# Differential attention: the near keys' bias block becomes the last of equal key blocks, and its maximum is taken negated

## The chip, the cores and the metric

The kernel runs on one core of a Trainium2 chip. The metric is the device time of one execution in microseconds; the time before is the median of three timed runs. A separate execution was taken with the hardware profiler, and all the rows shown come from it.

## What is computed

One inference step of a one-layer streaming encoder: a norm, one input projection, two groups of attention heads side by side, an output projection, an MLP with squared ReLU, a gated embedding and a final norm, for a prompt of 2048 tokens and a sample of 32 tokens with 128 cached keys. The change touches group A, the differential attention: 4 heads, each with two maps of 64 dimensions and values of 128.

```python
def diff_core(q, k, v, bias, mask, lam):
    s = jnp.einsum('bqhmd,bkhmd->bhmqk', q, k) * (HEAD_DIM ** -0.5) + bias[:, None]
    s = jnp.where(mask, s, NEG)
    p = jax.nn.softmax(s, axis=-1)
    w = p[:, :, 0] - lam * p[:, :, 1]
    return jnp.einsum('bhqk,bkhe->bqhe', w, v)
```

The mask lets a query see the keys of its own chunk of 64 and of all chunks before. The bias depends on the distance between key and query by buckets (T5), and far enough back all distances share the last bucket, so that there the bias is a constant that drops out of the softmax. The kernel subtracts that constant from the table once; what is left is zero for all keys but the nearest ones.

## The kernel before

**Precision by halves.** Operands are split into a high part and a rest (`hi`, `lo`), each product is three matmuls (`mm3`, L211 to L213), and the rest is computed by GpSimd (POOL, L174 and L184) or VectorE (DVE).

**Tiles.** Queries are taken in 16 tiles of 128 (`t`), two tiles to a pair (`attn_a_pair`). `attn_a` runs over the heads `g`, and for each head loads the bias tile `ba` (`bias_a`: 256 columns, one buffer, the visible corner masked by a POOL memset, L314) and the keys `ka`, then runs over its pairs. It is called four times in the program: twice in a first stretch for tiles 0 to 3 and then tiles 4 to 7 with the sample (`JA0`; `ka` has one buffer there), and twice in a second stretch for tiles 8 to 11 and 12 to 15 (`JA1`).

**Blocks.** The keys that tile `t` sees, 128 (t + 1) of them, are cut into blocks. The last 256 keys (128 for tile 0) are the near block, with the bias; the rest are far blocks of up to 512, as equal as multiples of 128 allow, without bias. For each block and each of the two maps `m`:

- PE computes the scores into one of three PSUM banks `s`, two matmuls, one for each half of q (L594).
- Far block: DVE takes the negated maximum straight from PSUM (L600), ACT the exponential from PSUM with that maximum as its bias, with the sum of the row accumulated in `z` (L608).
- Near block: DVE adds the bias, writes the sum to SBUF and takes the maximum in the same instruction (L603, with a second, short instruction that reads the maximum out), negates the maximum (L606), and ACT takes the exponential from SBUF (L608).

Then the maxima of the blocks are joined, if there is more than one (L613 to L624: a minimum, an exponential on ACT for each map, five short DVE instructions); each block of the second map is scaled by ACT (L630), and added to the first map's scaled block by DVE (L631). PE transposes the result in groups of four 128 x 128 pieces into PSUM (`tpp`, L666), ACT and DVE split it (`pH` L673, `pL` L674), and PE multiplies with the values (`o`, L680 to L682). A norm of the head's output follows (L684 to L694, with `ss` on PE).

**Order.** The instruction order of every engine comes from a scheduler that models the time of each instruction and fills an engine's gaps with later work: in the first stretch with projections (`vps`, `qps`) and the transposes of the prompt (`xp`), in the second with the MLP of the first half of the tokens (`ups`, `dps`; DVE adds `dps` into `h` at L982). The order is fixed in the program, and each engine runs its own in order. All transfers are issued in order from SP's queue (L165).

Of the kernel before, what the change touches and what calls it, by code (L numbers as in the profile page):

```python
# [12 lines left out]
F32 = mybir.dt.float32  # L13
F32R = mybir.dt.float32r
AF = mybir.ActivationFunctionType
ALU = mybir.AluOpType
# [3 lines left out]
P = 128  # L20
D = 1024
SP = 2048
SS = 32
T = SP + SS
PAST = 128
# [4 lines left out]
NEG = -1e30  # L30
# [121 lines left out]
class Kern:  # L152
# [155 lines left out]

    def bias_a(self, pool, h):
        nc = self.nc  # L310
        t = pool.tile([P, 256], F32, tag="ba", bufs=1, name="ba")
        src = self.dba[h, 127 : 127 + P * 383].rearrange("(p c) -> p c", c=383)[:, :256]
        self.dma(t, src)
        nc.gpsimd.memset(t[0:64, 192:256], NEG)  # L314
        return t

    def bias_b(self, pool, h):
# [235 lines left out]
    def attn_a_pair(self, g, j, kt, ba, pool, ps_s, ps_t, ps_o):  # L553
        nc = self.nc
# [9 lines left out]
        for qi, t in enumerate(tiles):  # L564
            if samp:
                nr = SS
                blocks = [(SP, PAST + SS, 0)]
                kb = SP
                nkeys = PAST + SS
            else:  # L570
                nr = P
                kb = 0
                nkeys = P * (t + 1)
                nfar = max(nkeys - 256, 0)
                nb = (nfar + 511) // 512
                blocks = []
                pos = 0
                for i in range(nb):
                    n = P * ((nfar // P - pos // P + nb - i - 1) // (nb - i))
                    blocks.append((pos, n, None))  # L580
                    pos += n
                blocks.append((nfar, nkeys - nfar, 256 - (nkeys - nfar)))
            nb = len(blocks)
            e = [
                pool.tile([P, 2048 if not self.small else 1024], F32, tag=f"e{m}", bufs=2 if m == 0 or self.small else 1, name="e")
                for m in range(2)
            ]
            nm = pool.tile([P, 2, 8], F32, tag="nm", bufs=2, name="nm")
            z = pool.tile([P, 2, 8], F32, tag="z", bufs=2, name="z")
            for bi, (k0, n, near) in enumerate(blocks):  # L590
                for m in range(2):
                    s = ps_s.tile([P, 512], F32, tag="s", name="s")[:nr, :n]
                    for hl in range(2):
                        nc.tensor.matmul(  # L594
                            s, q[:, m, hl, P * qi : P * qi + nr], kt[:, m, k0 - kb : k0 - kb + n], start=hl == 0, stop=hl == 1
                        )
                    dst = e[m][:nr, k0 - kb : k0 - kb + n]
                    nmx = nm[:nr, m, bi : bi + 1]
                    if near is None:
                        nc.vector.tensor_reduce(nmx, s, axis=AX.X, op=ALU.max, negate=True)  # L600
                        src = s
                    else:
                        nc.vector.tensor_tensor_reduce(  # L603
                            dst, s, ba[:nr, near : near + n], 1.0, -3e38, ALU.add, ALU.max, nmx
                        )
                        nc.vector.tensor_scalar(nmx, nmx, -1.0, None, op0=ALU.mult)  # L606
                        src = dst
                    nc.scalar.activation(dst, src, AF.Exp, bias=nmx, accum_out=z[:nr, m, bi : bi + 1])  # L608
            c = pool.tile([P, 2, 8], F32, tag="c", bufs=2, name="c")
            rz = pool.tile([P, 2], F32, tag="rz", bufs=2, name="rz")  # L610
            if nb > 1:
                gm = pool.tile([P, 2], F32, tag="gm", bufs=2, name="gm")
                nc.vector.tensor_reduce(gm[:nr], nm[:nr, :, :nb], axis=AX.X, op=ALU.min)  # L613
                for m in range(2):
                    nc.scalar.activation(
                        c[:nr, m, :nb], nm[:nr, m, :nb], AF.Exp, bias=gm[:nr, m : m + 1], scale=-1.0
                    )
                nc.vector.tensor_tensor(z[:nr, :, :nb], z[:nr, :, :nb], c[:nr, :, :nb], op=ALU.mult)
                nc.vector.tensor_reduce(rz[:nr], z[:nr, :, :nb], axis=AX.X, op=ALU.add)
                nc.vector.reciprocal(rz[:nr], rz[:nr])  # L620
                nc.vector.tensor_scalar(c[:nr, 0, :nb], c[:nr, 0, :nb], rz[:nr, 0:1], None, op0=ALU.mult)
                nc.vector.tensor_scalar(
                    c[:nr, 1, :nb], c[:nr, 1, :nb], rz[:nr, 1:2], self.nlam[:nr], op0=ALU.mult, op1=ALU.mult
                )  # L624
            else:
                nc.vector.reciprocal(c[:nr, :, 0], z[:nr, :, 0])
                nc.vector.tensor_scalar(c[:nr, 1, 0:1], c[:nr, 1, 0:1], self.nlam[:nr], None, op0=ALU.mult)
            for bi, (k0, n, near) in enumerate(blocks):
                sl = slice(k0 - kb, k0 - kb + n)
                nc.scalar.activation(e[1][:nr, sl], e[1][:nr, sl], AF.Copy, scale=c[:nr, 1, bi : bi + 1])  # L630
                nc.vector.scalar_tensor_tensor(  # L631
                    e[0][:nr, sl], e[0][:nr, sl], c[:nr, 0, bi : bi + 1], e[1][:nr, sl], op0=ALU.mult, op1=ALU.add
                )
            ws.append(e[0])
# [7 lines left out]
        for c0 in range(0, len(kts), 4):  # L642
# [16 lines left out]
            for qi, w in enumerate(ws):  # L659
                nr = SS if samp else P  # L660
# [984 lines left out]
```

## Time and profile before

| | |
|---|---|
| median of three timed runs | 3224.73 us (3218.4 to 3230.53) |
| profiled execution | 3224.94 us |
| its span (first to last instruction) | 3223.1 us |
| mean granted PE clock | 0.974 |
| busy: PE, DVE, ACT, POOL | 3019.3, 1813.4, 1791.5, 1768.7 us |
| score matmuls of group A (L594, prompt) | 768 |
| DVE maxima of far blocks (L600) | 256, 147.4 us |
| DVE bias and maximum of near blocks (L603) | 136, 53.7 us |
| negations (L606) | 136 |

A row of the grouped view reads: line, engine, operation, tile written <- tiles read, partitions x elements, count, then busy time in us and the mean in ns of one, then the idle time of the engine right before these instructions and which instruction ended it. A wait row reads: waiting instruction <- what ended the wait, total us, number of times, the longest. Matmuls are pipelined, and the length shown for one includes its way through the array, so what a matmul takes up is read from one start to the next.

### The profile page before, as it was taken

How to read it: one execution, taken by the hardware profiler on the slowest of the kernel's cores; microseconds unless marked ns; L12 is line 12 of the kernel's file. 1: busy time of each engine (PE TensorE's matmuls, PEld its weight loads, DVE VectorE, ACT ScalarE, POOL GpSimd, SP SyncE). 2: the span in 40 equal slices, each digit the busy share in tenths (PEclk: the TensorE clock that was granted, in tenths of full speed). 3: DMA queues.
4: the chain of work that ended last, by engine and by line, in shares of the span. 5: the costliest groups of instructions: out<-in, count | busy, mean ns of one | idle time of the engine just before them, and what ended most of it. 6: DMA issues, size and time to landing. Idle time of an engine off the chain costs nothing.

```text
span 3223.1 us, 51787 instructions
## 1 busy us (share of the span) xinstructions
PE 3019.3 (94%) x17497; PEld 2639.9 (82%) x17497; DVE 1813.4 (56%) x4270; ACT 1791.5 (56%) x3966; POOL 1768.7 (55%) x2451
## 2 busy tenths in 40 slices
PE   7989898999989999999999999998899999999997
PEld 6967788879878888788889999887788887888875
DVE  5126765444455454676675676235466665755845
ACT  4226665666566675676676776334354454444543
POOL 5427657443234544565564445657465567677751
PEclk9989899999999999999999999999999999999998
DMA  7578676987687854654564534456444468675611
GB/s 218 182 198 233 191 210 197 256 235 218 187 243 212 240 146 123 158 174 136 146 190 134 138 110 135 131 163 196 133 153 148 158 242 287 203 253 186 219 58 53
DMA packets 556257, 579.89 MB, mean 180 GB/s; under 512 B 41900, under 2 KB 412912, under 8 KB 555992
## 3 DMA queue, kind: packets, MB, share of 16 engines
q1 hardware_dynamic: 555992, 576.58, 59.7%
q8 instruction: 139, 2.28, 0.3%
q14 instruction: 126, 1.03, 0.1%
HBM read 438.37 MB, written 142.01 MB: 180 GB/s over the span
## 4 chain that ended last, share of the span: by engine, by line
PE 63%; DMA 11%; DVE 9%; ACT 4%; POOL 2%; issue 2%; SPq 1%; DVEq 0%; POOLq 0%; ACTq 0%
PE xps L211 3%; PE xps L212 3%; PE xps L213 3%; PE ups L211 3%; PE ups L212 3%; PE ups L213 3%; PE dps L211 3%; PE s L594 3%; PE dps L212 3%; PE dps L213 3%; PE dp L211 2%; PE dp L213 2%; PE dp L212 2%; PE ob L800 2%; PE gps L213 2%
## 5 line engine op out<-in xcount | busy, mean ns | idle before, releaser
L184 POOL TENSOR_TENSOR wl<-wr,wh 128x256 fp32r<-128x256 f32 x776 | 580.6, 780 | 463.3 <-ACT wh L189 405.4
L189 ACT ACTIVATE wh<-wr 128x1024 fp32r<-128x1024 f32 x258 | 272.6, 1057 | 259.4 <-PE dps L212 40.3
L211 PE MATMUL dps<-uh,wh 128*128 128x272 f32 (+1 forms) x768 | 265.4, 346 | 35.6 <-DVE h L982 27.7
L174 POOL TENSOR_TENSOR wl<-wr,wh 128x256 fp32r<-128x256 f32 x256 | 193.6, 787 | 170.5 <-ACT wh L189 170.3
L211 PE MATMUL ups<-cH,wh 128*128 128x272 f32 (+1 forms) x768 | 250.6, 327 | 2.7 <-ACT sqacc L913 1.5
L213 PE MATMUL dps<-uh,wl 128*128 128x272 f32 (+1 forms) x768 | 252.0, 328 | 0.0
L212 PE MATMUL dps<-ul,wh 128*128 128x272 f32 (+1 forms) x768 | 252.0, 328 | 0.0
L212 PE MATMUL ups<-cL,wh 128*128 128x272 f32 (+1 forms) x768 | 249.8, 325 | 1.2 <-POOL cL L174 1.2
L213 PE MATMUL ups<-cH,wl 128*128 128x272 f32 (+1 forms) x768 | 250.2, 326 | 0.0
L982 DVE TENSOR_TENSOR h<-h,dps 128x272 f32<-128x272 f32 (+1 forms) x384 | 195.9, 514 | 90.9 <-PE dps L213 88.7
L211 PE MATMUL qps<-aH,wh 128*128 128x512 f32 (+1 forms) x640 | 229.3, 358 | 8.8 <-DVE a L368 3.6
L213 PE MATMUL qps<-aH,wl 128*128 128x512 f32 (+1 forms) x640 | 229.0, 358 | 0.0
L212 PE MATMUL qps<-aL,wh 128*128 128x512 f32 (+1 forms) x640 | 228.5, 357 | 0.0
L594 PE MATMUL s<-ka,q 128*128 128x512 f32 (+3 forms) x768 | 188.9, 350 | 37.0 <-ACT e L608 19.3
L211 PEld LDWEIGHTS dps<-uh,wh 128*128 128x128 f32 x768 | 148.5, 193 | 60.6 <-DVE h L982 40.0
L608 ACT ACTIVATE e<-s,nm 128x384 f32<-128x384 f32 (+3 forms) x256 | 154.6, 609 | 64.5 <-DVE nm L600 42.6
L600 DVE TENSOR_REDUCE nm<-s 128x1 f32<-128x512 f32 (+3 forms) x256 | 147.4, 587 | 61.1 <-PE s L594 60.0
L212 PE MATMUL dp<-dx,dw 128*128 128x512 f32 x448 | 177.5, 396 | 0.7 <-DVE dx L195 0.7
L174 POOL TENSOR_TENSOR dw<-dv,dw 128x256 fp32r<-128x256 f32 x160 | 149.2, 961 | 49.1 <-ACT dw L189 39.8
L211 PE MATMUL dp<-dx,dw 128*128 128x512 f32 x448 | 174.7, 396 | 0.0
L594 PEld LDWEIGHTS s<-ka,q 128*128 128x128 f32 x768 | 128.3, 196 | 54.3 <-ACT e L608 24.3
L213 PE MATMUL dp<-dx,dw 128*128 128x512 f32 x448 | 171.5, 396 | 0.0
(273 smaller groups left out, 9593.9 us busy)
## 6 DMA issues: line engine op xcount, KB each, us to landing
wd<-w_down SPq DMA_DIRECT2D x96, 512.0 KB, 5.4
wr<-w_in SPq DMA_DIRECT2D x74, 512.0 KB, 5.5
q<-qS SPq DMA_DIRECT2D x256, 128.0 KB, 4.1
v<-vSa SPq DMA_DIRECT2D x64, 512.0 KB, 4.4
wr<-w_up SPq DMA_DIRECT2D x64, 512.0 KB, 4.3
wr<-w_down SPq DMA_DIRECT2D x64, 512.0 KB, 4.0
ut<-uS SPq DMA_DIRECT2D x56, 512.0 KB, 4.1
ka<-kS SPq DMA_DIRECT2D x32, 512.0 KB, 8.0
```

Of the source, the lines that this page charges most:

```text
L174: nc.gpsimd.tensor_tensor(out[:, sl], a[:, sl], b[:, sl], op=op)
L184: nc.gpsimd.tensor_tensor(out[:, sl], a[:, sl], b[:, sl], op=op)
L189: nc.scalar.activation(hi, raw, AF.Copy)
L211: nc.tensor.matmul(ps, lh, rh, start=start and i == 0, stop=False)
L212: nc.tensor.matmul(ps, lh, rl, start=False, stop=False)
L213: nc.tensor.matmul(ps, ll, rh, start=False, stop=stop and i == n - 1)
L594: nc.tensor.matmul(s, q[:, m, hl, P * qi : P * qi + nr], kt[:, m, k0 - kb : k0 - kb + n], start=hl == 0, stop=hl == 1)
L600: nc.vector.tensor_reduce(nmx, s, axis=AX.X, op=ALU.max, negate=True)
L608: nc.scalar.activation(dst, src, AF.Exp, bias=nmx, accum_out=z[:nr, m, bi : bi + 1])
L800: nc.tensor.matmul(o[:, qa:qb], vt, pt[:kn, i - kfirst, qa:qb], start=x == 0 and y == 0, stop=x == len(order) - 1 and y == 1,)
L982: nc.vector.tensor_tensor(hv, hv, ps, op=ALU.add)
```

## The change

Three edits. The near block is no longer a block of its own of 256 keys: all the keys of a tile are cut into equal blocks of up to 512, and the last of them is the one with the bias. The bias tile grows to 512 columns, its first half zero, set by one more POOL memset; a last block of n keys uses its last n columns. A tile of 512 keys or fewer has one block, and nothing to join.

Per head the blocks of the 16 tiles go from 1, 1, 2, 2, 2, 2, 3, 3, 3, 3, 4, 4, 4, 4, 5, 5 to 1, 1, 1, 1, 2, 2, 2, 2, 3, 3, 3, 3, 4, 4, 4, 4. The near blocks are 128, 256, 384, 512, 256, 384, 384, 512, 384, 384, 384, 512, 384, 384, 384 and 512 wide.

The instruction that adds the bias now also multiplies by -1 and takes the minimum, so that the negated maximum comes out of it, and the separate negation goes. What it writes has its sign turned, which the exponential undoes with a scale of -1.

```diff
     def bias_a(self, pool, h):
-        t = pool.tile([P, 256], F32, tag="ba", bufs=1, name="ba")
+        t = pool.tile([P, 512], F32, tag="ba", bufs=1, name="ba")
         src = self.dba[h, 127 : 127 + P * 383].rearrange("(p c) -> p c", c=383)[:, :256]
-        self.dma(t, src)
-        nc.gpsimd.memset(t[0:64, 192:256], NEG)
+        self.dma(t[:, 256:], src)
+        nc.gpsimd.memset(t[:, :256], 0.0)
+        nc.gpsimd.memset(t[0:64, 448:512], NEG)
         return t
...
-                blocks = [(SP, PAST + SS, 0)]
+                blocks = [(SP, PAST + SS, 256)]
...
-                nfar = max(nkeys - 256, 0)
-                nb = (nfar + 511) // 512
+                nb = (nkeys + 511) // 512
                 blocks = []
                 pos = 0
                 for i in range(nb):
-                    n = P * ((nfar // P - pos // P + nb - i - 1) // (nb - i))
-                    blocks.append((pos, n, None))
+                    n = P * ((nkeys // P - pos // P + nb - i - 1) // (nb - i))
+                    blocks.append((pos, n, None if i < nb - 1 else 512 - n))
                     pos += n
-                blocks.append((nfar, nkeys - nfar, 256 - (nkeys - nfar)))
...
                         nc.vector.tensor_tensor_reduce(
-                            dst, s, ba[:nr, near : near + n], 1.0, -3e38, ALU.add, ALU.max, nmx
+                            dst, s, ba[:nr, near : near + n], -1.0, 3e38, ALU.add, ALU.min, nmx
                         )
-                        nc.vector.tensor_scalar(nmx, nmx, -1.0, None, op0=ALU.mult)
                         src = dst
-                    nc.scalar.activation(dst, src, AF.Exp, bias=nmx, accum_out=z[:nr, m, bi : bi + 1])
+                    nc.scalar.activation(
+                        dst, src, AF.Exp, bias=nmx, scale=1.0 if near is None else -1.0,
+                        accum_out=z[:nr, m, bi : bi + 1],
+                    )
```

Since the scheduler places every instruction anew, the order of all engines moves between the first stretch and the end of the second.

## Prediction

> **What bounds the kernel now.** I read the page first (PE is busy for 94% of the span), then the busy time by stage, then who waited for whom on PE inside the two stages that the change touches. Keys and queries of the differential attention meet in two stretches: heads over tiles 0 to 7 from 222 to 505 us, and over tiles 8 to 15 from 1283 to 1960 us. The busy times of these stages (columns as in the header):
>
> ```profile
> core 0: us, PE busy (x) PEld busy (x) DVE busy (x) ACT busy (x) POOL busy (x), PEclk, DMA share, GB/s
> 222.00:505.00 283.00, 243.82 (x1635) 222.47 (x1636) 199.67 (x680) 192.06 (x593) 168.98 (x258) 0.93 0.76 211
> 1283.00:1960.00 677.00, 644.18 (x3962) 576.90 (x3962) 451.44 (x1047) 461.52 (x1111) 359.85 (x517) 0.98 0.53 147
> ```
>
> PE idles 39 us of 283 in the first and 33 of 677 in the second, while DVE and ACT, the engines that the change relieves, are at two thirds. So the attention is not bound by DVE or ACT: projections and the MLP, scheduled between its steps, keep PE going. What DVE and ACT save reaches the end of the span only through PE's waits. Those of the first stretch, largest first (total us, times, longest):
>
> ```profile
> PE s L594 <- DMA q<-qS: 8.7, 5, 3.6
> PE s L594 <- DMA ka<-kS: 8.4, 2, 4.4
> PE tpp L666 <- DVE e L631: 6.8, 7, 2.2
> PE s L594 <- ACT e L608: 5.2, 8, 1.4
> PE ss L691 <- DVE sh L191: 3.3, 2, 2.0
> PE tpp L666 <- DVE pL L674: 3.2, 2, 2.0
> ```
>
> And of the second:
>
> ```profile
> PE s L594 <- ACT e L608: 14.1, 8, 6.2
> PE dps L211 <- DVE h L982: 9.8, 17, 1.6
> PE o L681 <- DVE pL L674: 3.3, 1, 3.3
> PE dps L211 <- ACT relu L947: 3.1, 3, 2.4
> ```
>
> Two kinds stand there. Loads of q and k: 17.1 us. Waits that end on DVE or ACT: 18.5 us in 19 waits in the first stretch, 30.3 us in 29 in the second, together **48.8 us in 48 waits**. That is all that the change can shorten directly.
>
> **The change part by part.**
>
> *Matmuls.* Per head the 16 tiles have 48 blocks before and 40 after. Times 4 heads, 2 maps and 2 halves that is 128 fewer score matmuls (768 to 640), but the key columns are the same. Does a matmul cost by itself? PE's rows in order of time, from start to next start:
>
> ```profile
> 1940.62 0.40 PE L594 MATMUL s<-ka,q 128*128 128x256 f32 x2
> 1940.85 0.28 PE L680 MATMUL o<-pH,v 128*128 128x256 f32 x1
> ...
> 1941.27 0.27 PE L681 MATMUL o<-pL,v 128*128 128x128 f32 x1
> 1941.38 0.27 PE L682 MATMUL o<-pH,v 128*128 128x128 f32 x1
> ...
> 1946.42 0.63 PE L594 MATMUL s<-ka,q 128*128 128x512 f32 x2
> 1946.89 0.29 PE L211 MATMUL dps<-uh,wh 128*128 128x272 f32 x1
> ```
>
> Two of 256 columns occupy 0.23 us, two of 512 occupy 0.47: 0.45 and 0.46 ns a column, nothing left per matmul. I take 0 for the 128. The bound from the other side is the 128-column row: 0.11 us where its columns are worth 0.06, so 0.05 each, 6.6 us at most; a loss is excluded, as no column is added. The Trainium skill, "TensorE: Matmul & The Clock Gate", section "Back-to-back issue gap", gives a sustained 81 ns at 128 columns and 131 ns at 512, that is some 64 ns that do not depend on width; by it 128 matmuls would be an estimated 8 us. The two pairs above speak against it.
>
> *DVE and ACT.* The durations, by shape (count, then total us and mean ns); L763 is the band attention's instruction of the same kind as L603, and shows widths that L603 does not have yet:
>
> ```profile
> L600 DVE TENSOR_REDUCE nm<-s 128x1 f32<-128x512 f32 x104 | 69.8, 683 | 19.4 <-PE s L594 18.8
> L600 DVE TENSOR_REDUCE nm<-s 128x1 f32<-128x384 f32 x128 | 69.6, 549 | 39.9 <-PE s L594 39.5
> L603 DVE CUSTOM_DVE_ANT_0 e<-s,ba 128x256 f32<-128x256 f32 x120 | 49.0, 418 | 38.4 <-PE s L594 30.2 <-POOL ba L314 4.2 <-issue 2.1
> L606 DVE TENSOR_SCALAR nm<-nm 128x1 f32<-128x1 f32 x128 | 17.9, 147 | 1.0
> L631 DVE SCALAR_TENSOR_TENSOR e<-e,c 128x512 f32<-128x512 f32 x52 | 43.4, 856 | 8.7 <-ACT e L630 8.7
> L631 DVE SCALAR_TENSOR_TENSOR e<-e,c 128x256 f32<-128x256 f32 x68 | 44.6, 663 | 2.3 <-ACT e L630 2.1
> L608 ACT ACTIVATE e<-s,nm 128x512 f32<-128x512 f32 x104 | 70.9, 684 | 27.7 <-DVE e L631 13.7 <-DVE nm L600 13.3 <-DVE rz L619 0.2
> L608 ACT ACTIVATE e<-e,nm 128x256 f32<-128x256 f32 x120 | 60.5, 505 | 38.4 <-DVE nm L606 38.2
> L608 ACT ACTIVATION_READ_ACCUMULATOR e<-s,nm 128x1 f32 x256 | 51.4, 201 | 0.0
> ```
>
> ```profile
> L763 DVE CUSTOM_DVE_ANT_0 eb<-sb,bb 128x512 f32<-128x512 f32 x8 | 5.5, 685 | 8.0 <-PE tpb L775 6.1 <-PE sb L760 1.9
> L763 DVE CUSTOM_DVE_ANT_0 eb<-sb,bb 128x384 f32<-128x384 f32 x8 | 4.4, 544 | 0.4 <-PE tpb L775 0.4
> ```
>
> A near block costs what a far one of its width does (685 against 683 ns), so biasing zeros is free on DVE. After the change 128 far reductions are 512 wide and 64 are 384 wide; before 104 and 128, and 24 narrower ones that I leave out: 128 x 0.683 + 64 x 0.549 - 139.4 = -16.8 us. The 120 near ones of 256 become 72 of 384, 32 of 512 and 16 of 256: 39.2 + 21.9 + 6.7 - 49.0 = +18.8. The negation (L606) goes: -17.9. L631 runs over 32 fewer blocks; its part that does not depend on width is 2 x 663 - 856 = 470 ns: -15.0. DVE: about -31 us. ACT loses 64 exponentials with their accumulator reads: 64 x (201 + a fixed part of 2 x 505 - 684 = 326 ns) = -34 us. L630's 32 come on top, uncounted. Together 65 us, a twentieth of the two engines' 1305 us in the two stretches. Two thirds busy, they keep most of that as more idle time.
>
> What the order makes of it on DVE, first head, tiles 2 and 3 (e,nm<-s,ba is the near block, its second row reads out the maximum). Before:
>
> ```order
> L603 ISA e,nm<-s,ba 128x256
> L603 ISA nm 128x1
> L627 TENSOR_SCALAR c<-c,nlam 128x1
> L600 TENSOR_REDUCE nm<-s 128x1 x2
> L606 TENSOR_SCALAR nm<-nm 128x1
> ```
>
> After, where lines stand one lower or higher:
>
> ```order
> L602 ISA e,nm<-s,ba 128x256
> L602 ISA nm 128x1
> L632 SCALAR_TENSOR_TENSOR e<-e,c 128x128
> L602 ISA e,nm<-s,ba 128x384
> L602 ISA nm 128x1
> L627 RECIPROCAL c<-z 128x2
> ```
>
> Tile 2 has become one block of 384 a map: its far reductions and its negation are gone, and so is the joining of two blocks' maxima.
>
> *What PE sees.* Each of the 48 waits ends on a chain that starts with a block's hand-off PE to DVE to ACT. One in six hand-offs goes (64 of 384), and I let the waits go with them: 48.8 / 6 = 8.1 us. Of the 40 waits left 128 in 320 stand behind a near block and lose the 0.147 us of L606: 2.4 us. Tiles 2 and 3 no longer join two blocks, which lies on the chain at the first heads:
>
> ```profile
> 222.13 0.66 PE s L594 x2
> ...
> 233.47 0.38 ACT c L615 x2
> ...
> 234.83 5.04 DMA ka<-kS
> ...
> 239.96 1.08 PE s L594 x4
> ```
>
> That is the first head's 12 us from its first score to the next head's k load, which must wait since k has one buffer there; two joins of 0.38 us in each of the two heads that stand uncovered: 1.5 us. **Sum: 12.0 us.** Its bounds are 0 (every wait is set by the order or by loads) and 50.3 (all of the 48.8 and the 1.5).
>
> *Loads and POOL.* In the first stretch the order moves. On PE, around the second head's last score (the s row), before:
>
> ```order
> L691 MATMUL ss<-sh,ones_r 128x256
> L213 MATMUL vps<-wh,aL 128x256
> L692 MATMUL ss<-sl,ones_r 128x256
> L594 MATMUL s<-ka,q 128x256 x2
> L211 MATMUL vps<-wh,aH 128x256
> L212 MATMUL vps<-wl,aH 128x256
> ```
>
> and so on for some fifty rows of projections (vps, qps) to the third head's first score. After, from the second head's last score (the first row) to the third head's first (the last row):
>
> ```order
> L593 MATMUL s<-ka,q 128x512 x2
> L667 MATMUL tpp<-ident,e 128x128 x2
> L692 MATMUL ss<-sh,ones_r 128x256
> L693 MATMUL ss<-sl,ones_r 128x256
> L667 MATMUL tpp<-ident,e 128x128 x3
> L593 MATMUL s<-ka,q 128x128 x4
> ```
>
> Three heads now run back to back, and the projections follow them. The same PE work is done in another order, so I cost this at 0: the heads' own chain is shorter, and the projections moved behind cover later switches. What it costs if that cover fails is a rival below. POOL gets 16 more memsets of the bias tile, each waiting for DVE's last near block of the head before (the tile has one buffer); weight splits queue behind it. Before, the existing memset waited for the bias load, which waited for the same release and then for its transfer, and the two lists above hold no wait of PE on POOL. I take 0.
>
> The profiled execution took 3224.94 us (its span is 3223.1), the median of the three timed runs is 3224.73, so the sum needs no shift: 3224.9 - 12.0 = **3213 us**.
>
> **The rivals.** A change of 0.5%, 16.1 us, is about what a measurement here can tell from none.
>
> *Wider hand-offs eat the gain.* A near block of 512 holds its hand-off 685 - 418 - 147 = 120 ns longer on DVE and 684 - 505 = 179 ns on ACT. If all 48 waits stood behind such blocks that is 14.4 us back: 3227, no change. For it: the engines are not saturated, so what counts is latency and not work. Against it: only 32 of 128 near blocks are that wide. The Trainium skill, "Perfetto Trace Analysis", section "Optimizing Scalar/DVE Operations", says this of engines that are not saturated but cause bubbles elsewhere: smaller instructions may let work complete sooner. The stage rows above show that case. 3219 to 3231, chance 0.20.
>
> *The waits shrink faster than the work.* If half of the 48.8 us goes, with the 1.5: 3224.9 - 25.9 = 3199. For it: PSUM banks of near blocks come free after DVE, not after ACT, and the score matmuls' wait on ACT is the largest single one (19.3 us in both lists). Against it: half of the 64 block passes that go lie in the second stretch, where DVE and ACT do 913 of the 1305 us, so their load falls little there. 3191 to 3208, chance 0.23.
>
> *A matmul has a price of its own* (the 0.05 us above): 6.6 us more, 3206, chance 0.03. The rule on the issue gap would come out near it.
>
> *Uncovered k loads, slower.* Seven head switches in the first stretch each need k loaded after the last score. Landing took 5.04 us above, and the median is longer:
>
> ```profile
> ka<-kS SPq DMA_DIRECT2D x32, 512.0 KB, 8.0
> ```
>
> Exposed in full, 7 x 8.0 = 56 us stand where PE pays 17.1 for q and k now: +38.9 - 12.0, 3252. It makes the kernel measurably slower once a switch costs (17.1 + 12.0 + 16.1) / 7 = 6.5 us. For it: the order above, with nothing but the attention's own steps between heads. Against it: the first two heads are hardly covered today either, and heads 5 to 8 get what moved. 3236 to 3260, chance 0.14.
>
> **How the numbers follow.** The forecast, 3213 with 3205 to 3221 of its own, has 0.40. Faster by over 0.5% means below 3208.8: the second rival, most of the third, and a quarter of the forecast: 0.36. Slower means above 3241.0: 0.12, the last rival but for its low end. The rest, 0.52, is no change. The range 3192 to 3238 leaves out the far ends of the second and the last rival, some 0.15.
>
> **What would show it.** Right: L606 gone, the far blocks' exponentials down from 256 to 192, DVE about 31 and ACT 34 us less; waits on DVE and ACT near 38 us in the two stretches; a pair of 512-wide scores still 0.47 us. Wrong: if the stretches shorten but the rest of the span grows by as much, PE's order and not the waits set the end; if waits on ka and q rise above 17 us by tens, the loads took over; if near blocks of 512 cost well over 685 ns on DVE, the price list is wrong.

## The result, and the profile after

The changed kernel takes 3207.03 us (median of 7 runs, 3204.4 to 3214.37) against 3224.73 (7 runs, 3218.4 to 3232.9): a ratio of 0.995, 95% interval 0.9932 to 0.9968, 16 to 18 us less. The forecast was 3213. The profiled execution took 3204.4 us (span 3202.6; before 3224.94 and 3223.1).

The size is near the forecast, so the first question is whether it came from where the forecast put it. The busy times of the two attention stretches, at the same times as before:

```profile
222.00:505.00 283.00, 246.67 (x1613) 222.78 (x1612) 189.72 (x557) 185.86 (x521) 174.94 (x273) 0.93 0.77 211
1283.00:1960.00 677.00, 649.32 (x4002) 583.62 (x4002) 443.48 (x959) 462.41 (x1065) 367.76 (x537) 0.98 0.52 148
```

PE is busy for 2.9 us more in the first and 5.1 us more in the second, 8 of the 20.5 us by which the span is shorter. Then PE's waits in the first stretch, largest first (total us, times, longest):

```profile
PE s L593 <- DMA q<-qS: 9.0, 5, 3.6
PE tpp L667 <- DVE e L632: 7.4, 7, 2.8
PE s L593 <- DMA ka<-kS: 7.1, 2, 4.3
PE s L593 <- DVE nm L602: 3.7, 3, 2.6
PE ss L692 <- DVE c L627: 2.3, 1, 2.3
PE o L682 <- DVE pL L675: 2.1, 1, 2.1
PE s L593 <- ACT e L606: 1.7, 3, 0.9
```

And in the second:

```profile
PE s L593 <- ACT e L606: 16.0, 9, 6.5
PE dps L211 <- DVE h L983: 8.6, 12, 3.0
PE dps L211 <- ACT relu L948: 7.6, 3, 5.7
```

The rows shown that end on DVE or ACT add up to 17.2 + 32.2 = 49.4 us. The forecast's 48.8 left out the rows under 3 us of its lists, so the two sums are not of the same rows: with every such row of both lists the waits went from 54.3 to 51.7 us, 2.6 less where the forecast had 10.5. The loads of q and k take 16.1 us, where they took 17.1. So most of what the forecast paid for is not to be seen in this pair, although the time went down.

The prices are as forecast (DVE and ACT, count, total us and mean ns):

```profile
L599 DVE TENSOR_REDUCE nm<-s 128x1 f32<-128x512 f32 x128 | 86.6, 684 | 18.4 <-PE s L593 17.7
L632 DVE SCALAR_TENSOR_TENSOR e<-e,c 128x512 f32<-128x512 f32 x80 | 63.8, 824 | 6.1 <-ACT e L631 6.0
L602 DVE CUSTOM_DVE_ANT_0 e<-s,ba 128x384 f32<-128x384 f32 x72 | 39.0, 552 | 32.8 <-PE s L593 29.1 <-PE tpp L667 3.2 <-DMA ka<-kS 0.6
L602 DVE CUSTOM_DVE_ANT_0 e<-s,ba 128x512 f32<-128x512 f32 x32 | 21.9, 687 | 14.6 <-PE s L593 12.3 <-PE tpp L667 1.9
L602 DVE CUSTOM_DVE_ANT_0 e<-s,ba 128x256 f32<-128x256 f32 x16 | 6.5, 418 | 1.5 <-POOL ba L315 0.7 <-PE s L593 0.6
```

The near block with -1 and min costs what it cost with 1 and max (418 ns at 256 columns), a 512 wide one 687 (685 forecast), and DVE waited 0.7 us in all for POOL's new memsets. L606's negation is gone. Matmuls of 512 columns, PE's rows in order of time:

```profile
1863.59 0.62 PE L593 MATMUL s<-ka,q 128*128 128x512 f32 x2
1864.06 0.28 PE L211 MATMUL dps<-uh,wh 128*128 128x272 f32 x1
...
1864.80 1.09 PE L593 MATMUL s<-ka,q 128*128 128x512 f32 x4
1865.72 0.29 PE L211 MATMUL dps<-uh,wh 128*128 128x272 f32 x1
```

Two take 0.47 us and four 0.92, 0.45 ns a column as before.

Where did the time come from? I took PE's pure work (each matmul's columns at 0.45 ns, 0.11 us at least; 2862 us in all) and noted by how much PE's rows in order of time stand behind it; waits and a lower clock both count as standing behind. The three heads that now run back to back cost at first. Before:

```profile
222.00:262.00 40.00, 29.91 (x170) 26.76 (x171) 23.86 (x112) 25.56 (x89) 13.37 (x21) 0.77 0.84 213
262.00:300.00 38.00, 35.95 (x188) 29.42 (x187) 23.97 (x80) 22.02 (x63) 30.11 (x45) 1.00 0.86 245
```

After:

```profile
222.00:262.00 40.00, 25.09 (x118) 20.03 (x117) 25.17 (x92) 24.70 (x75) 14.92 (x25) 0.74 0.85 216
262.00:300.00 38.00, 32.61 (x174) 28.12 (x173) 19.23 (x53) 19.18 (x47) 24.50 (x37) 0.87 0.79 206
```

PE is busy 8.2 us less in these 78 us and its clock lower; at 200 us of pure work the changed kernel stands 13.6 us further behind than before. By 300 that is made up, by 500 it leads by 3.0, by 1100 by 18.7, by 1900 by 22.0, and at the end by 19.8. Most of the gain so falls between 500 and 1100 us of pure work, some 630 to 1290 us of the span. There the band attention, the projections and the start of the MLP run, none of which the change touches. PE's largest waits at 505 to 1100 us before:

```profile
PE sb L760 <- DVE stb L763: 6.3, 7, 1.9
PE ops L211 <- ACT oact L189: 5.6, 2, 4.0
PE qps L211 <- DVE a L368: 3.6, 1, 3.6
PE qps L211 <- ACT kn L473: 3.6, 2, 3.2
```

After:

```profile
PE tpb L776 <- DVE pLb L786: 4.4, 3, 2.4
PE vps L211 <- DVE a L369: 3.6, 2, 2.1
PE sb L761 <- DVE stb L764: 3.5, 7, 0.9
```

The instructions here are the same in both kernels, only in another order. That gave a theory to set against the forecast's. **Shorter chains**: the gain is what the two stretches' hand-offs save. **Order**: the gain is mostly another order of the same work, which the change happened to bring. **Engine work**: DVE's and ACT's savings count in full.

### The profile page after: what moved, and what is told of

It reads as the page before. It is cut to its first block, busy times and chain, and to the rows that moved or that the text cites. A ratio compares the mean times of both kernels' runs of the same rounds, so it can differ in the third digit from the quotient of the medians.

```text
span 3202.6 us, 51162 instructions
## 1 busy us (share of the span) xinstructions
PE 3013.9 (94%) x17369; PEld 2632.1 (82%) x17369; DVE 1765.2 (55%) x4006; ACT 1762.2 (55%) x3790; POOL 1764.8 (55%) x2467
## 4 chain that ended last, share of the span: by engine, by line
PE 51%; DMA 5%; DVE 5%; ACT 2%; issue 1%; POOL 1%; SPq 1%; DVEq 0%; POOLq 0%; ACTq 0%
PE xps L211 3%; PE dps L211 3%; PE xps L212 3%; PE xps L213 3%; PE ups L212 3%; PE ups L211 3%; PE ups L213 3%; PE dps L212 3%; PE dps L213 3%; PE s L593 2%; PE dp L211 2%; PE dp L212 2%; PE dp L213 2%; PE gps L213 2%; PE gps L212 2%; PE gps L211 2%
## 5 line engine op out<-in xcount | busy, mean ns | idle before, releaser
L593 PE MATMUL s<-ka,q 128*128 128x512 f32 (+3 forms) x640 | 180.7, 384 | 39.3 <-ACT e L606 17.7
L764 DVE CUSTOM_DVE_ANT_0 eb<-sb,bb 128x320 f32<-128x320 f32 (+2 forms) x232 | 103.9, 478 | 125.6 <-PE tpb L776 113.7
L211 PE MATMUL vps<-wh,aH 128*128 128x256 f32 (+1 forms) x544 | 159.2, 294 | 12.4 <-DVE rsv L223 4.1
L675 DVE TENSOR_TENSOR pL<-tpp,pH 128x512 fp32r<-128x512 f32 (+5 forms) x168 | 95.2, 585 | 124.1 <-ACT pH L674 123.3
```

Of the source, the lines that this page charges most:

```text
L211: nc.tensor.matmul(ps, lh, rh, start=start and i == 0, stop=False)
L593: nc.tensor.matmul(s, q[:, m, hl, P * qi : P * qi + nr], kt[:, m, k0 - kb : k0 - kb + n], start=hl == 0, stop=hl == 1)
L675: nc.vector.tensor_tensor(l_, s_, h_.bitcast(F32), op=ALU.subtract)
L764: nc.vector.tensor_tensor_reduce(e[:, w * i : w * i + w], s, bb[:nr, b0 + w * i : b0 + w * i + w], 1.0, -3e38, ALU.add, ALU.max, st[:, 3 + ...
```

## The experiments

All ratios are against the kernel before, run beside each.

**The change in parts.** The negation alone (old blocks):

```diff
-dst, s, ba[:nr, near : near + n], 1.0, -3e38, ALU.add, ALU.max, nmx
+dst, s, ba[:nr, near : near + n], -1.0, 3e38, ALU.add, ALU.min, nmx
...
-nc.vector.tensor_scalar(nmx, nmx, -1.0, None, op0=ALU.mult)
...
-nc.scalar.activation(dst, src, AF.Exp, bias=nmx, accum_out=z[:nr, m, bi : bi + 1])
+nc.scalar.activation(dst, src, AF.Exp, bias=nmx, scale=1.0 if near is None else -1.0, accum_out=z[:nr, m, bi : bi + 1])
```

> The old blocks; only the negation is taken into the near blocks' instruction, so L606 is gone. Shorter-chain theory (each wait of PE is as long as the hand-offs it ends on): 128 of 384 hand-offs lose 0.147 us, so 48 x 128 / 384 x 0.147 = 2.4 us less, 3222 us, and PE's waits on DVE and ACT fall a little in both attention stretches. Order theory (most of the measured 17.7 us came because the program's instructions fell into another order, and PE's stalls between 505 and 1100 us went with it): the order moves here too, so anything from 3205 to 3232 is possible, and the difference lies in 505 to 1100 us and not in the attention stretches. Engine-work theory (what DVE saves counts in full): 17.9 us less, 3207.

Measured (e1): 3193.44 us, ratio 0.9918 (0.9895 to 0.9942). That is 26 us less: more than the whole change, and more than the 19.0 us (17.9 and the sample's 1.1) of DVE instructions that it takes away. DVE's busy time did not even fall (1815.0 us for 1813.4), as other rows grew: the instruction that combines the two maps (L631) took 148.3 us for 141.7.

The blocks alone are the change without these lines.

> The new blocks and the wide bias tile, but the negation stays an instruction of its own. Shorter-chain theory: 8.1 us from the 64 hand-offs fewer and 1.5 from the joins of tiles 2 and 3, so 3215 us; scaled up to the measured gain, 3210 to 3213. Order theory: anything from 3203 to 3232, not to be had by subtracting the first experiment from the whole change. Engine-work theory: 31 - 18 = 13 us of DVE and 34 of ACT, at most 13 us on the path, 3212.

Measured (e2): 3202.84 us, 0.9943 (0.9924 to 0.9962).

The blocks in one stretch alone (here the first; for the second the condition is `not self.small`):

```diff
+if self.small:
     nb = (nkeys + 511) // 512
...
+else:
+    nfar = max(nkeys - 256, 0)
...
+    blocks.append((nfar, nkeys - nfar, 512 - (nkeys - nfar)))
```

> The new blocks in the first attention stretch alone (tiles 0 to 7); tiles 8 to 15 keep the old ones, and the negation is merged in both. Shorter-chain theory: 18.5 x 32 / 128 = 4.6 us for the hand-offs, 1.5 for the joins, 2.4 for the negation: 3216 us. Order theory: the first stretch decides what runs beside it and what is left for 505 to 1100 us, so nearly the whole gain should come with it: 3205 to 3210, with the gain again in 505 to 1100 us.

Measured (e3): 3204.74 us, 0.9952 (0.9935 to 0.9969).

> The new blocks in the second attention stretch alone (tiles 8 to 15); tiles 0 to 7 keep the old ones, and the negation is merged in both. Shorter-chain theory: 30.3 x 32 / 256 = 3.8 us for the hand-offs and 2.4 for the negation: 3219 us, with the gain in 1283 to 1960 us. Order theory: the stretch from 505 to 1100 us then behaves as in the kernel before or in the one with the negation alone, whichever has the same order there; 3-4 us from the second stretch itself on top.

Measured (e4): 3212.66 us, 0.9974 (0.9959 to 0.9988).

The parts do not add up. By the ratios the negation gives -26 us and the blocks -18, together -45, where the change gives -16. On top of the merged negation, the blocks cost 11 us in the first stretch, 18 in the second and 10 in both. A theory in which each edit has a price of its own does not give this. Engine work as the source of the gain falls too: the negation alone gave more than it took off DVE. Shorter chains expected 3222, 3215, 3216 and 3219, and were missed by 29, 12, 11 and 6 us.

**The same work in another order.** Two edits that remove and add no instruction, each in the kernel before and in the changed one. The first issues the second map's scores first (of PE's 15,569 rows in order of time it moves about as many as the change: 3080 lines of difference against 3355):

```diff
-                for m in range(2):
+                for m in (1, 0):
                     s = ps_s.tile([P, 512], F32, tag="s", name="s")[:nr, :n]
```

> The kernel before with its two maps' scores issued in the other order (second map first): the same work, another order of the program on all engines. Shorter-chain theory: nothing changes in number or length of the hand-offs, 3225 us within 3. Order theory: the time scatters by 5 to 15 us, 3210 to 3240, and the difference shows where the order of the projections and the band attention fell out differently, in 505 to 1100 us.

Measured (e5): 3197.65 us, 0.9908 (0.9887 to 0.9929).

The second swaps the last two products of the output:

```diff
-nc.tensor.matmul(oo, v[:kn, x, 0], pL[:kn, x, q0:nq], start=False, stop=False)
-nc.tensor.matmul(oo, v[:kn, x, 1], pH[:kn, x, q0:nq], start=False, stop=last)
+nc.tensor.matmul(oo, v[:kn, x, 1], pH[:kn, x, q0:nq], start=False, stop=False)
+nc.tensor.matmul(oo, v[:kn, x, 0], pL[:kn, x, q0:nq], start=False, stop=last)
```

> The kernel before with the product of the low values and the high weights (L682) issued ahead of that with the low weights (L681): the same work, the last product waits for the low weights one matmul later. Shorter-chain theory: up to 3.3 + 2.1 us of o's waits on pL may go, 3220 to 3225. Order theory: 3210 to 3240.

Measured (e6): 3198.64 us, 0.9912 (0.9882 to 0.9942).

The same two in the changed kernel:

> The changed kernel with the second map's scores first. Shorter-chain theory: 3207 us within 3. Order theory: 3200 to 3225, and part of the lead over the kernel before may be gone.

Measured (e7): 3197.41 us, 0.991 (0.989 to 0.9931).

> The changed kernel with the product of the low values ahead of that with the low weights. Shorter-chain theory: 3202 to 3207 us, as in the same edit of the kernel before. Order theory: 3200 to 3225, with another difference than the same edit makes to the kernel before.

Measured (e8): 3194.56 us, 0.9904 (0.9882 to 0.9926).

Each reordering makes the kernel before 28 to 30 us faster (by the ratios), nearly twice what the change gave. So the kernel before has an order that is bad for it, and leaving it is worth more than the change. It could still be that each edit takes away a cost of its own. Both edits together tell that apart:

> The kernel before with both edits of order at once (second map first; the product of the low values ahead of that with the low weights): a fourth order of the old blocks. Theory that the kernel before has an unlucky order, and that the change by itself is worth little: near the other two reordered ones, 3192 to 3207 us. Theory that the two edits each take away a cost of their own (some 27 us each): well below 3190, down to 3171.

Measured (e9): 3199.8 us, 0.9929 (0.9902 to 0.9957). No further gain: the edits are not prices that add, and I read them as other draws of the order. That both take away one and the same cost is not excluded by this run alone; e1, which has neither edit, comes out as low.

> The changed kernel with both edits of order at once: a fourth order of the new blocks. Unlucky-order theory: 3190 to 3205 us, so that old and new blocks differ by under 5 us in three orders of four. If the new blocks are worth the 12 us of the forecast by themselves, this one should come out 12 us below its counterpart with the old blocks.

Measured (e10): 3193.1 us, 0.9905 (0.9881 to 0.993). It beats both kernels: with e5, e7 and e8 it is one of four whose interval lies wholly below that of the change.

> The old blocks with the negation merged and the second map's scores first: another order of the kernel with the negation alone, which took 3193 us. If the merged negation is what makes that one fast (a chain shorter by 0.147 us, or 17.9 us of DVE), this one stays at 3193 within 4 us or below the reordered kernel before by as much. Unlucky-order theory: 3190 to 3210, no pattern.

Measured (e11): 3205.25 us, 0.9939 (0.992 to 0.9958). The merged negation, 26 us faster in one order, is 10 us slower than its counterpart e5 in the other. Its 3193 was an order, not its price.

The order theory missed too, in size and in place. Seven runs came out faster than the ranges that it gave: e1, e5 and e6 by 11 to 12 us, e8 by 5, e7 by 3, e2 and e3 by less than 1. And the lead was not only in the band attention and projections: of the 28 us by which e5 and e6 end ahead of the kernel before (table below), 13 and 11 are there at 1100 us of pure work; the rest comes after that, by 1900. Old and new blocks were to differ by under 5 us in three orders of four; they do in two.

**Longer hand-offs.** The negation seven times:

```diff
 nc.vector.tensor_scalar(nmx, nmx, -1.0, None, op0=ALU.mult)
+nc.vector.tensor_scalar(nmx, nmx, -1.0, None, op0=ALU.mult)
...
+nc.vector.tensor_scalar(nmx, nmx, -1.0, None, op0=ALU.mult)
```

> The kernel before with the negation of the near blocks' maxima done seven times instead of once (an odd number of sign changes, so the values stay): six more instructions of 0.147 us, 0.88 us, in each of 128 of the 384 hand-offs, 107 us more work on DVE. Shorter-chain theory (each wait behind a near hand-off grows by as much as the hand-off): 48 x 128 / 384 = 16 waits x 0.88 = 14.1 us, 3221 us from the mean of three orders of the old blocks (3207), 3239 from the kernel before. Engine-work theory: up to 107 us more. If the hand-offs' length isn't on the path at all: 3195 to 3225, within the scatter of the orders.

Measured (e12): 3278.1 us, 1.0167 (1.0141 to 1.0193): +54 us against the kernel before, +81 against the mean of its three reorderings. Both the 14 us of the shorter-chain sum and "not on the path" fall. The negations cost what they should on DVE (the sample's eight are in the counts; the third column is the idle time before them):

```profile
L606 DVE TENSOR_SCALAR nm<-nm 128x1 f32<-128x1 f32 (+1 forms) x136 | 19.5, 147 | 1.0
...
L612 DVE TENSOR_SCALAR nm<-nm 128x1 f32<-128x1 f32 (+1 forms) x136 | 19.6, 148 | 1.4
```

and of the six new ones' 117 us 54 to 81 reached the end, which is within what engine work allowed (up to 107). Most of it is lost at one place. The busy times of the last stretch of the second attention, in this run:

```profile
1990.00:2031.00 41.00, 38.08 (x278) 35.59 (x276) 29.23 (x92) 29.14 (x73) 19.95 (x30) 1.00 0.32 99
2031.00:2082.00 51.00, 23.97 (x112) 18.32 (x113) 24.62 (x80) 23.16 (x60) 7.83 (x12) 0.68 0.20 61
```

and its waits there:

```profile
PE tpp L672 <- DVE e L637: 9.0, 2, 5.5
PE ops L211 <- ACT oact L189: 8.6, 1, 8.6
PE s L594 <- ACT e L614: 4.9, 5, 1.9
```

In the 41 us up to 2031 PE is busy for 93%, with the longer hand-offs. Then the MLP's matmuls that covered them are used up, the last head stands alone, and PE is busy for 24 of 51 us at a clock of 0.68. DVE is busy for under half of these 51 us, so it is the chain and not DVE's load that holds PE there. The kernel before still had MLP matmuls beside its last head and behind its last score, at 1960 us:

```profile
1960.00:2000.00 40.00, 40.00 (x325) 40.00 (x325) 20.43 (x42) 23.42 (x51) 24.10 (x37) 1.00 0.44 134
```

Of the 60 us that this kernel ends further behind its pure work than the kernel before, 37 arise between 1740 and 1800 us of work, in this tail; 9 before 500 and 11.5 between 500 and 1100. In the other thirteen kernels the last score stands at 1651 to 1716 us of pure work, in this one at 1760. It was run in one order only, so how much of the tail is the length of the hand-offs and how much the order that the scheduler made of them is not separated.

**All orders side by side.** How many us PE stands behind its pure work when it has done 500, 1100 and 1900 us of it, and at its end (2860). 1100 is near the start of the second stretch, 1900 behind its end:

```
                               500   1100   1900   2860
old blocks   before          132.6  191.8  277.0  343.3
             e5 (m)          127.4  179.2  246.0  315.7
             e6 (o)          120.9  181.2  245.9  315.8
             e9 (m, o)       129.1  169.9  243.3  315.3
             e1 (neg)        125.4  170.4  243.4  311.3
             e11 (neg, m)    135.3  181.3  252.7  323.8
first new    e3              133.5  182.6  253.3  326.2
second new   e4              128.6  182.3  259.8  330.6
new blocks   after           129.6  173.1  255.0  323.5
             e2 (blocks)     123.8  167.8  253.5  325.2
             e7 (m)          133.2  173.5  243.0  315.3
             e8 (o)          132.6  182.2  245.1  312.3
             e10 (m, o)      139.1  187.9  244.0  309.2
seven        e12             141.4  212.1  329.9  403.3
```

Up to 1100, the six kernels with new blocks in the first stretch lose 177.9 us on average (168 to 188), the seven with old ones 179.4 (170 to 192). From 1100 to 1900, the six with new blocks in the second lose 72.3 (56 to 86), the seven with old ones 72.2 (65 to 85). Between the two kinds of blocks there is no difference that this scatter lets one see. The kernel before is the worst of its seven in both columns, 12 us above the mean in the first and 13 in the second.

One row shows what an order changes, and what it does not. PE's wait for the exponentials in the second stretch was 14.1 us before and 16.0 after. In e5, the kernel before with the maps exchanged:

```profile
PE dps L211 <- DVE h L982: 9.4, 10, 5.4
PE s L594 <- ACT e L608: 8.2, 3, 6.6
```

and in e10, whose second stretch begins earlier, at 1257 us, one wait of this kind is left, ahead of that window:

```profile
PE s L593 <- ACT e L606: 7.3, 1, 7.3
```

In thirteen of the fourteen kernels (not in e3) one such wait of 3.7 to 7.3 us stands 16 to 19 us behind the second stretch's first score, with old and new blocks. What comes and goes is the rest: 7.9 us before, 9.5 after, 1.6 in e5, none in e10. That it goes with how many scores happen to stand without other matmuls around them is my reading; I did not count them.

All of PE's waits that end on DVE or ACT, taken in each kernel from its own first to its own last score of each stretch, are 54.3 us in the kernel before and 37.2, 41.9 and 42.1 in e5, e6 and e9; in the changed kernel they are 50.1, and 22.2, 38.3 and 38.2 in e7, e8 and e10. Among equal work they lie up to 28 us apart. The means, 43.9 and 37.2, differ by 6.7 us, so it can't be told from these runs whether the change shortens the waits by the forecast's 10.5 us or not at all.

**The change by itself**, with the order's luck averaged: the four pairs of equal edits differ by ratio by -0.0050 (as given), +0.0002 (m), -0.0008 (o) and -0.0024 (both), in us -16.1, +0.6, -2.6 and -7.7. Their mean is -6.5, with a 95% interval of some 12 us to either side from their own scatter; without the pair as given, whose kernel before is the outlier, it is -3.2. What the change is worth by itself is so not settled; zero lies well inside the interval, and no other pair repeats the 16 us. The part of the order is clearer: the kernel before stands 27 us above the mean of its three reorderings, the changed one 14 above its own. Which waits make the kernel before so slow stays open, as its loss against e5 and e6 is spread over both halves of the table.

## Why the prediction came out near, and where its working was wrong

The time was forecast 6 us too high and lies in the range. That it came so near was luck: the mechanism that was to make the time is not shown to have made it.

- *What bounds the kernel* held. PE's cover decides, not DVE or ACT: DVE lost 48 us and ACT 29 of busy time, and the time does not follow these numbers (in e1 DVE's busy time stayed and the time fell by 26 us).
- *DVE and ACT prices.* ACT came out near (29 us for 34). DVE lost 48 for 31, and two things make up most of the difference. The 24 narrower far reductions go altogether (8.6 us), and the combining step saved 20 us for 15. A 512 wide near exponential took 723 ns for 684. None of this can be found again in the time.
- **The step that failed** is "One in six hand-offs goes (64 of 384), and I let the waits go with them", 8.1 us, with the 2.4 of the negation. With every row counted, the waits on DVE and ACT went from 54.3 to 51.7 us in the pair as given, 2.6 less for 10.5. Waits of this kind are not a fixed share of the hand-offs: with not one hand-off fewer or shorter, e5, e6 and e9 have 12 to 17 us less of them than the kernel before. And 20 of the 48 waits, 12.9 us, did not end on a block's hand-off at all: there the MLP's `dps` waited for its own `h` (L982) and `relu` (L947), and these rows came to 16.2 us after. An effect of the size forecast, averaged over orders, is neither shown nor excluded.
- *The joins* (1.5 us) could not be told from the rest: three heads now stand back to back, and the place they were read from is gone.
- *Matmuls at 0* held: 0.47 us for a pair of 512. The Trainium skill's "TensorE: Matmul & The Clock Gate", section "Back-to-back issue gap", would have made the 128 fewer ones worth an estimated 8 us; no row of 256 to 512 columns here shows such a part. PE's busy time did fall by 5.4 us, but e6, with the matmuls of the kernel before, has 17 us less than it, so that is no price either.
- **"The same PE work is done in another order, so I cost this at 0"** is the other step. For the change's own three heads it was nearly right: 13.6 us lost, all made up by 300 us of work. As a price for a new order it was far off: orders of the same work lie 27 us apart (3197.65 to 3224.73), more than the 21 us that the range reached below the forecast. The text had the test for it ("if the stretches shorten but the rest of the span grows"), but the other sign came: the rest shrank.
- *The rivals.* Wider hand-offs are not seen to eat the gain, as blocks old and new lose alike within the scatter. Uncovered k loads were seen at the first heads, but the waits for q and k stayed at 16 us, so the later switches were covered, as the forecast had argued. "The waits shrink faster" had the direction of the gain right, and its cause is not shown. What no rival named was that the time of before is itself one draw of the order.
- *POOL's memsets at 0* held.

The near hit is so the sum of two things: a change whose own worth is not settled (3 to 7 us less by the means, with an interval that holds 0), and an order that happened to be some 13 us less unlucky than the one it replaced. A forecast of 12 us with a loss or gain of order up to 27 us beside it could as well have come out far off.

## What to carry to other kernels

Where a scheduler sets the order, as here, a difference under 1% between two versions says little about the edit: reorder both without changing their work (exchange two symmetric loops or two commuting products) three or four times and compare the means. Do this for the kernel before as well; here it was the outlier. And read a wait with its cover: what was saved on a covered chain could not be seen in the time here, while lengthening it cost where the work beside it ran out, in e12 mostly at one place, the last head, and not evenly.

## What the runs showed that was not expected

- Time against the length of a hand-off looks steep on one side. Six negations more (0.88 us in each of 128 near hand-offs) cost 54 us against the kernel before and 81 against its reorderings, the largest part in one tail of 51 us; one negation fewer cannot be seen among the orders. The six were run in one order only.
- In that tail PE's granted clock was 0.68 with PE busy for 24 of 51 us, 1.00 in the 41 us ahead of it and 0.93 behind it:

```profile
2082.00:2120.00 38.00, 35.76 (x179) 30.20 (x178) 18.85 (x33) 13.92 (x20) 19.08 (x26) 0.93 0.59 193
```

  The heads back to back showed the same at 222 to 262 us (0.74 with PE busy for 25.1 of 40 us). So in these rows the clock is low where PE idles for want of cover.
